# Bias rows of ada_b as single rows in zeroed tiles instead of 32 copies each

## The chip, the core and the metric

The kernel runs on one core of one Trainium2 chip. Its engines are TensorE (PE, with its weight loads PEld), VectorE (DVE), ScalarE (ACT), GpSimd (POOL) and SyncE (SP), which here issues every DMA. The metric is device time in microseconds (us) of one execution; the median of several executions is compared.

## What is computed

Two layers of a diffusion backbone, with 256 latent tokens and 256 context tokens of width 1024. Each layer is a half-step SwiGLU network, a token mixer (neighbourhood attention in layer 0, a short gated convolution in layer 1) and a second half-step network; the context is only carried as far as the attention needs it. Every sub-layer takes its shift, scale and gate from a modulation vector of the layer:

```
s_c, s_cc = silu(c), silu(c_ctx)
m  = (s_c  @ ada_w[i] + ada_b[i])        # 9 rows of 1024 for the latent tokens
mc = (s_cc @ ada_w[i] + ada_b[i])        # the same for the context
x  = layer_norm(alpha * x + w * gate * f(x * (1 + scale) + shift)) * g + b
```

`ada_w[i]` is 1024 x 9216 and `ada_b[i]` has 9216 entries, all in float32. The change is about how `ada_b` gets to the core.

## The kernel before

Matrices stream from DRAM in tiles, and each is split into a high part (ScalarE, line 178) and a low part (VectorE, line 181); three matmuls on these parts make one product. The order of TensorE's instructions is that of the program. The instructions of the other engines, and with them SP's queue of DMAs, are put in order by a planner at build time: it goes by the order in the text, shifted by the `high_priority` offsets, and by what it reckons to be ready.

The first modulation (rows 0 and 1 of layer 0) is worked out in `start_step`, before anything else can run, in five steps `(k0, n)` over column blocks of 128: (0, 1), (1, 1), (2, 2), (4, 2), (6, 2). A step loads its part of `ada_w` into tiles `ar` (line 478), loads x and the context (`x`, `xc`, line 485) when `k0` is even, multiplies by the silu of the two vectors (`ada`, line 490; `cst` holds the two vectors in columns 0 and 1 of 32, the others are zero), adds the bias tile `ab0` (`rows`, line 495), transposes x (`xT`, line 500), turns the rows into columns by a matmul with the selector `sel` (`mc`, line 522) and applies the modulation (lines 509 to 515). Between the pieces of a step stand the matmuls of the first panels of the network's first matrix (`f`, lines 537 to 539), whose tiles `w1r` are loaded at line 175.

`ab0` is two tiles of 128 x 512, cleared on VectorE (line 450). Half of the bias is loaded in step 0 and half in step 3, each time behind the step's last `ar` (line 481). Each of two rows of 512 entries is copied 32 times, to fill 64 partitions. The selector adds partitions 32m + v and 64 + 32m + v, for row m and vector v.

The other modulations are worked out beside the networks by `ada` (line 224), a background generator that is advanced by `tick`, a fraction of a step for each group of matmuls. A group has one or two vectors. For each of eight blocks of `ada_w`, VectorE multiplies and adds into the accumulators `acc` (lines 241 and 243); then the bias comes into `adab` (line 249), four ticks of work later TensorE sums over the partitions (line 259), VectorE adds the bias (line 260), and the result goes to the DRAM rows `scr` (line 262). From there `fold_cols` fetches it as `mrow`, and other code as `gate`. In `ada` too each of the two half rows of a vector is copied 32 times. The tag `acc` has four buffers of 512 columns, shared with `ab0` at the start; `adab` has one buffer.

Of the kernel before, what the change touches and what calls it, by code (L numbers as in the profile page):

```python
# [9 lines left out]
F32 = mybir.dt.float32  # L10
F32R = mybir.dt.float32r
AF = mybir.ActivationFunctionType
ALU = mybir.AluOpType
# [3 lines left out]
P = 128  # L17
D = 1024
# [46 lines left out]
def backbone_kernel(  # L65
# [6 lines left out]
    nc = tc.nc  # L72
    sync = nc.sync
# [7 lines left out]
    hp = phase.__enter__()  # L81
# [6 lines left out]
    def nm(s):  # L88
        uid[0] += 1
        return f"{s}_{uid[0]}"  # L90

    def act(dt=F32, s="a"):
        return ap.tile([P, 512], dt, tag="act", name=nm(s))
# [7 lines left out]
    def tpb(s="tp"):  # L101
        return bank("tp", s)
# [85 lines left out]
    def wpair(w, u, c0, c1, s):  # L188
        if c1 == c0 + 256:
# [22 lines left out]
    nc.vector.memset(ones, 1.0)  # L212
    sel = cp.tile([P, 4], F32, tag="sel", name="sel")
    idv = ident.rearrange("p (o m e) -> p o m e", o=2, m=2)
    nc.vector.tensor_tensor(out=sel.rearrange("p (m v) -> p m v", m=2), in0=idv[:, 0, :, 0:2],
                            in1=idv[:, 1, :, 0:2], op=ALU.add)
    win_sb = cp.tile([P, 64], F32, tag="wmask", name="wmask")
    rope = cp.tile([P, 2, 4, HD], F32, tag="rope", name="rope")

    scr = [tc.dram_tile([2, 9 * D], F32, name=f"scr{i}") for i in range(2)]  # L220
    xscr = tc.dram_tile([2 * P, D], F32, name="xscr")


    def ada(vecs):


        acc = {}
        for l, m in dict.fromkeys((l, m) for l, m, _ in vecs):
            for k in range(KC):
                w = hp.tile([P, D], F32, tag="ar", bufs=3, name=nm("ar"))  # L230
                sync.dma_start(w, ada_w[l, k * P:(k + 1) * P, m * D:(m + 1) * D])
                for i, vec in enumerate(vecs):
                    if vec[:2] != (l, m):
                        continue
                    if k == 0:
                        acc[i] = [hp.tile([P, 512], F32, tag="acc", bufs=4, name=nm("acc")) for _ in range(2)]
                    sc = cst[:, k, vec[2]:vec[2] + 1]
                    for h in range(2):
                        src, a = w[:, h * 512:(h + 1) * 512], acc[i][h]
                        if k == 0:  # L240
                            nc.vector.tensor_scalar(a, src, sc, None, op0=ALU.mult)
                        else:
                            nc.vector.scalar_tensor_tensor(out=a, in0=src, scalar=sc, in1=a,  # L243
                                                           op0=ALU.mult, op1=ALU.add)
                yield 1
        n = 2 * len(vecs)
        bt = hp.tile([P, 512], F32, tag="adab", name=nm("adab"))
        for i, (l, m, v) in enumerate(vecs):
            sync.dma_start(bt[64 * i:64 * i + 64],
                           bass.AP(ada_b.tensor, ada_b.offset + (l * 9 + m) * D, [[512, 2], [0, 32], [1, 512]]))  # L250
        yield 1
        yield 1
        yield 1
        rows = hp.tile([P, 512], F32, tag="adar", name=nm("adar"))
        ps = tpb("ada")
        for i in range(len(vecs)):
            for h in range(2):
                j = 2 * i + h
                nc.tensor.matmul(ps[32 * j:32 * j + 32, :], ones, acc[i][h], start=True, stop=True)
        nc.vector.tensor_tensor(out=rows[:32 * n], in0=ps[:32 * n], in1=bt[:32 * n], op=ALU.add)  # L260
        for i, (l, m, v) in enumerate(vecs):
            sync.dma_start(scr[l][v, m * D:(m + 1) * D].rearrange("(a b) -> a b", b=512),
                           rows[64 * i:64 * i + 64:32, :])
        yield 1

    def stream(*groups):
        for g in groups:
            yield from ada(g)
# [176 lines left out]


    w_in, w_out = ffn_w_in[0, 0], ffn_w_out[0, 0]
    ab0 = [hp.tile([P, 512], F32, tag="acc", bufs=4, name=nm("ab0")) for _ in range(2)]
    for h in range(2):
        nc.vector.memset(ab0[h], 0.0)  # L450
    xt = []
    for t in range(4):
        if t < 2:
# [9 lines left out]
    def start_tile():  # L463
        nar[0] += 1
        if nar[0] % 5 in (2, 4):
            return hp.tile([P, 2, 512], F32, tag="pt", bufs=4, name=nm("ar")).rearrange("p a b -> p (a b)")
        return hp.tile([P, D], F32, tag="ar", bufs=3, name=nm("ar"))

    def start_step(k0, n):

        ps = tpb("ada")
        m = n * P
        kt = 512 // m
        last = KC // kt - 1
        for a in range(KC // kt):
            w = start_tile().rearrange("p (k m c) -> p k m c", k=kt, m=2)
            for i in range(2):
                sync.dma_start(w[:, :, i], bass.AP(ada_w.tensor, ada_w.offset + a * kt * P * 9 * D + i * D + k0 * P,
                                                   [[9 * D, P], [P * 9 * D, kt], [1, m]]))
            if a == last and k0 % 4 == 0:  # L480
                sync.dma_start(ab0[k0 // 4][0:64], bass.AP(ada_b.tensor, ada_b.offset + k0 * P, [[D, 2], [0, 32], [1, 512]]))
            if a == (last if k0 else XAT) and k0 % 2 == 0:
                for t in range(4):
                    src = x[0] if t < 2 else ctxt[0]
                    sync.dma_start(xt[t][k0 // 4][:, k0 % 4 * P:k0 % 4 * P + 256],
                                   src[(t % 2) * P:(t % 2 + 1) * P, k0 * P:k0 * P + 256])
            for i in range(kt):
                for j in range(2):
                    o = 64 * (i % 2) + 32 * j
                    nc.tensor.matmul(ps[o:o + 32, 0:m], cst[:, a * kt + i, :], w[:, i, j, :],  # L490
                                     start=(a == 0 and i < 2), stop=(a == last and i >= kt - 2))
            if (a + 1) % (n if n == 1 else 2) == 0:
                yield
        rows = sp.tile([P, 256], F32, tag="s2", bufs=S2, name=nm("rows"))
        nc.vector.tensor_tensor(out=rows[:, 0:m], in0=ps[:, 0:m], in1=ab0[k0 // 4][:, k0 % 4 * P:k0 % 4 * P + m], op=ALU.add)

        def xT(k):
            px = tpb("xT")
            for t in range(4):
                nc.tensor.transpose(px[:, t * P:(t + 1) * P], xt[t][k // 4][:, (k % 4) * P:(k % 4 + 1) * P], ident)  # L500
            return px

        def mod(k, px):
            t = sp.tile([P, 512], F32, tag="s2", bufs=S2, name=nm("h"))
            hi, lo = act(F32R, "h0h"), act(F32R, "h0l")
            with tc.high_priority(offset=W_EARLY):
                for v in range(2):
                    s = slice(v * 256, (v + 1) * 256)
                    nc.scalar.activation(hi[:, s], px[:, s], AF.Identity, bias=mcol[:, k, 0, v:v + 1],
                                         scale=mcol[:, k, 1, v:v + 1])  # L510
                for v in range(2):
                    s = slice(v * 256, (v + 1) * 256)
                    nc.vector.tensor_scalar(t[:, s], px[:, s], mcol[:, k, 1, v:v + 1], mcol[:, k, 0, v:v + 1],
                                            op0=ALU.mult, op1=ALU.add)
                nc.vector.tensor_tensor(out=lo, in0=t, in1=hi.bitcast(F32), op=ALU.subtract)
            hT0.append((hi, lo))

        px = xT(k0)
        yield
        pc = tpb("mc")  # L520
        for i in range(n):
            nc.tensor.matmul(pc[:, 4 * i:4 * i + 4], rows[:, i * P:(i + 1) * P], sel, start=True, stop=True)
        pv = pc[:, 0:4 * n].rearrange("p (k m v) -> p k m v", k=n, m=2)
        nc.vector.tensor_copy(mcol[:, k0:k0 + n, 0, :], pv[:, :, 0, :])
        nc.vector.tensor_scalar(mcol[:, k0:k0 + n, 1, :], pv[:, :, 1, :], 1.0, None, op0=ALU.add)
        mod(k0, px)
        yield
        if n > 1:
            mod(k0 + 1, xT(k0 + 1))
            yield  # L530
# [23 lines left out]
    b1 = [mmb("f0", z) for z in range(2)]  # L554
    steps = ((0, 1), (1, 1), (2, 2), (4, 2), (6, 2))
    run(start_step(*steps[0]))
    for q, (k0, n) in enumerate(steps):
        nxt = start_step(*steps[q + 1]) if q < 4 else iter(())
        for g in range(6):
# [6 lines left out]
            p, j, z = g // 4, g // 2 % 2, g % 2  # L566
# [295 lines left out]
    hp = phase.__enter__()  # L862
# [67 lines left out]
    hTs, later = box  # L930
    phase = tc.tile_pool(name="ph2", bufs=1)
    hp = phase.__enter__()
    ext[0] = 3

    set_background(stream([(1, 1, 0), (1, 2, 0)], [(1, 3, 0)]), 0.35)
# [122 lines left out]
```

## Time and profile before

| what | value |
| --- | --- |
| median of 3 runs | 1293.48 us (1292.49 to 1294.41) |
| profiled execution | 1290.21 us |
| its span, first to last instruction | 1288.4 us |
| granted TensorE clock | 0.996 |
| DMA traffic | 271.26 MB, mean 211 GB/s |
| loads of `ab` | 2 of 128 KB |
| loads of `adab` | 19 of 128 KB |

The span leaves out what lies before the first and behind the last instruction, 1.8 us here. In the profile's rows, `L481` is a line of the kernel, `out<-in` names tiles and tensors without their numbers, `xN` is a count, and what stands in brackets or behind `<-` is the idle time ahead of it and what ended it. SPq rows are the issues of DMAs on SP, and their duration is that of the issue, not of the transfer.

### The profile page before, as it was taken

What the parts mean: (1) busy time and instruction counts of PE and PEld (TensorE: products, weight loads), DVE (VectorE), ACT (ScalarE), POOL (GpSimd) and SP (SyncE); (2) the same over time, 40 slices, a digit from 0 to 9 for tenths busy, and PEclk for the clock granted to TensorE, in tenths of its full rate; (3) what the DMA queues carried; (4) which work ended last, traced back from release to release, by engine and by line L of the source; (5) the groups of instructions that cost most, each with busy time, mean ns of one, the idle gap of its engine ahead of it and who ended that gap; (6) DMA issues with size and microseconds to landing.
All of it is one profiled execution on the core that took longest, in us unless ns stands there. A gap on an engine that the chain in (4) does not pass through costs nothing.

```text
span 1288.4 us, 17192 instructions
## 1 busy us (share of the span) xinstructions
PE 1256.5 (98%) x5890; PEld 1005.4 (78%) x5890; DVE 954.7 (74%) x1683; ACT 591.0 (46%) x1148; POOL 40.4 (3%) x69
## 2 busy tenths in 40 slices
PE   7999999999999999988999999999999999999997
PEld 4787778788778877766787787887788877788886
DVE  3599877595658767788997888867878688855545
ACT  2433132412326456677554535645435645655431
POOL 0000000000001111120000000000000000000000
PEclk9999999999999999989999999999999999999999
DMA  9978668484622744464998988677887764676641
GB/s 285 284 238 260 187 187 289 153 299 150 216 66 85 217 90 90 92 149 130 314 333 267 325 315 298 205 220 222 290 298 244 211 218 147 214 213 187 226 158 50
DMA packets 204018, 271.26 MB, mean 211 GB/s; under 512 B 30028, under 2 KB 149300, under 8 KB 203930
## 3 DMA queue, kind: packets, MB, share of 16 engines
q1 hardware_dynamic: 203930, 270.16, 66.9%
q8 instruction: 46, 0.75, 0.2%
q14 instruction: 42, 0.34, 0.1%
HBM read 267.93 MB, written 2.17 MB: 210 GB/s over the span
## 4 chain that ended last, share of the span: by engine, by line
PE 81%; DVE 7%; DMA 6%; ACT 3%; issue 1%; SPq 1%; POOL 0%; DVEq 0%; ACTq 0%
PE w L156 15%; PE w L157 14%; PE w L159 14%; PE f L537 6%; PE f L539 6%; PE f L538 6%; DMA w1r<-in_ffn_w_in_dram 4%; DVE w1l L181 2%; PE wkv L156 2%; PE wkv L159 2%; PE wkv L157 2%; PE wc L156 2%; PE wc L157 2%; PE wc L159 2%; DMA ar<-in_ada_w_dram 1%
## 5 line engine op out<-in xcount | busy, mean ns | idle before, releaser
L178 ACT ACTIVATE w1h<-w1r 128x512 fp32r<-128x512 f32 x352 | 203.1, 626 | 185.7 <-PE w L159 71.4
L181 DVE TENSOR_TENSOR w1l<-w1r,w1h 128x512 fp32r<-128x512 f32 x352 | 227.6, 685 | 66.7 <-ACT w1h L178 63.5
L156 PE MATMUL w<-w1h,hTh 128*128 128x512 f32 x528 | 210.8, 399 | 3.3 <-ACT hTh L105 3.3
L243 DVE SCALAR_TENSOR_TENSOR acc<-ar,cst,acc 128x512 f32<-128x512 f32 x266 | 187.5, 746 | 33.6 <-DMA ar<-in_ada_w_dram 33.3
L157 PE MATMUL w<-w1l,hTh 128*128 128x512 f32 x528 | 207.0, 392 | 0.0
L156 PE MATMUL w<-w2h,gh 128*128 128x512 f32 (+1 forms) x446 | 175.4, 394 | 0.0
L157 PE MATMUL w<-w2l,gh 128*128 128x512 f32 (+1 forms) x446 | 173.4, 389 | 0.0
L178 ACT ACTIVATE w2h<-w2r 128x512 fp32r<-128x512 f32 x176 | 101.5, 624 | 140.9 <-PE w L159 122.2
L159 PE MATMUL w<-w1h,hTl 128*128 128x512 f32 x528 | 163.4, 391 | 0.7 <-DVE hTl L106 0.7
L181 DVE TENSOR_TENSOR w2l<-w2r,w2h 128x512 fp32r<-128x512 f32 x176 | 114.0, 686 | 42.1 <-ACT w2h L178 41.4
L537 PE MATMUL f<-h0h,w1h 128*128 128x512 f32 x352 | 139.3, 396 | 0.0
L539 PE MATMUL f<-h0l,w1h 128*128 128x512 f32 x352 | 137.8, 392 | 0.0
L538 PE MATMUL f<-h0h,w1l 128*128 128x512 f32 x352 | 137.8, 391 | 0.0
L159 PE MATMUL w<-w2h,gl 128*128 128x512 f32 (+1 forms) x446 | 136.3, 387 | 0.0
L156 PEld LDWEIGHTS w<-w1h,hTh 128*128 128x128 f32 x528 | 99.2, 188 | 27.2 <-ACT hTh L105 4.6
L159 PEld LDWEIGHTS w<-w1h,hTl 128*128 128x128 f32 x528 | 98.9, 188 | 23.9 <-DVE hTl L106 1.5
L157 PEld LDWEIGHTS w<-w1l,hTh 128*128 128x128 f32 x528 | 99.2, 188 | 20.3 <-DVE w1l L181 0.3
L156 PEld LDWEIGHTS w<-w2h,gh 128*128 128x128 f32 x446 | 83.7, 188 | 21.8 <-issue 1.7
L159 PEld LDWEIGHTS w<-w2h,gl 128*128 128x128 f32 x446 | 83.3, 188 | 18.8
L157 PEld LDWEIGHTS w<-w2l,gh 128*128 128x128 f32 x446 | 83.7, 188 | 17.4
L537 PEld LDWEIGHTS f<-h0h,w1h 128*128 128x128 f32 x352 | 66.2, 188 | 17.9 <-issue 4.1
L539 PEld LDWEIGHTS f<-h0l,w1h 128*128 128x128 f32 x352 | 66.2, 188 | 14.4
(176 smaller groups left out, 1703.1 us busy)
## 6 DMA issues: line engine op xcount, KB each, us to landing
w1r<-in_ffn_w_in_dram SPq DMA_DIRECT2D x352, 256.0 KB
ar<-in_ada_w_dram SPq DMA_DIRECT2D x128, 512.0 KB
w2r<-in_ffn_w_out_dram SPq DMA_DIRECT2D x88, 512.0 KB
ar<-in_ada_w_dram SPq DMA_DIRECT2D x32, 256.0 KB
wkvr<-in_na_w_qkv_dram SPq DMA_DIRECT2D x32, 256.0 KB
wcr<-in_sc_w_in_dram SPq DMA_DIRECT2D x32, 256.0 KB
wqr<-in_na_w_qkv_dram SPq DMA_DIRECT2D x8, 512.0 KB
bias<-in_na_rpb_dram SPq DMA_DIRECT2D x64, 64.0 KB
```

Source lines behind the costliest of these rows:

```text
L156: nc.tensor.matmul(ps, lh, rh, start=first and i == 0, stop=False)
L157: nc.tensor.matmul(ps, lh, rl, start=False, stop=False)
L159: nc.tensor.matmul(ps, ll, rh, start=False, stop=last and i == n - 1)
L178: nc.scalar.activation(hi[:, a:a + m // W_HI], raw[:, a:a + m // W_HI], AF.Copy)
L181: nc.vector.tensor_tensor(out=lo[:, a:b], in0=raw[:, a:b], in1=hi[:, a:b].bitcast(F32), op=ALU.subtract)
L243: nc.vector.scalar_tensor_tensor(out=a, in0=src, scalar=sc, in1=a, op0=ALU.mult, op1=ALU.add)
L537: nc.tensor.matmul(ps, lh, hT0[k][0], start=(k == 0), stop=False)
L538: nc.tensor.matmul(ps, ll, hT0[k][0], start=False, stop=False)
L539: nc.tensor.matmul(ps, lh, hT0[k][1], start=False, stop=(k == KC - 1))
```

## The change

- `ab0` is one tile of 128 x 1024 with one clear. One DMA ahead of the loop over `start_step` puts bias row 0 into partition 2 and bias row 1 into partition 34, 1024 entries each. The loads at line 481 go.
- `sel` gets a second addition, by which partition 32m + 2 is added for both vectors. The matmul's rows 32m + 2 are zero, since column 2 of `cst` is zero, so what stands there is the bias alone.
- In `ada`, the bias goes into partitions 64i and 64i + 32 only, a row of 512 entries each. The tile `adab` is made and cleared (on GpSimd) once for each of the two phases that run `ada`, and is then used by all their groups.
- The accumulators, and `ab0` with them, are tiles of 1024 columns with two buffers, where there were four of 512.

```
+    sv = sel.rearrange("p (m v) -> p m v", m=2)
+    nc.vector.tensor_tensor(out=sv, in0=idv[:, 0, :, 0:2], in1=idv[:, 1, :, 0:2], op=ALU.add)
+    nc.vector.tensor_tensor(out=sv, in0=sv, in1=idv[:, 0, :, 2:3].to_broadcast([P, 2, 2]), op=ALU.add)
...
+    bias_rows = []
...
-                        acc[i] = [hp.tile([P, 512], F32, tag="acc", bufs=4, name=nm("acc")) for _ in range(2)]
+                        a = hp.tile([P, D], F32, tag="acc", bufs=2, name=nm("acc"))
+                        acc[i] = [a[:, 0:512], a[:, 512:D]]
...
-        bt = hp.tile([P, 512], F32, tag="adab", name=nm("adab"))
+        if not bias_rows:
+            bias_rows.append(hp.tile([P, 512], F32, tag="adab", name=nm("adab")))
+            nc.gpsimd.memset(bias_rows[0], 0.0)
+        bt = bias_rows[0]
         for i, (l, m, v) in enumerate(vecs):
-            sync.dma_start(bt[64 * i:64 * i + 64],
-                           bass.AP(ada_b.tensor, ada_b.offset + (l * 9 + m) * D, [[512, 2], [0, 32], [1, 512]]))
+            sync.dma_start(bt[64 * i:64 * i + 64:32], ada_b[l, m * D:(m + 1) * D].rearrange("(a b) -> a b", b=512))
...
-    ab0 = [hp.tile([P, 512], F32, tag="acc", bufs=4, name=nm("ab0")) for _ in range(2)]
-    for h in range(2):
-        nc.vector.memset(ab0[h], 0.0)
+    ab0 = hp.tile([P, D], F32, tag="acc", bufs=2, name="ab0")
+    nc.vector.memset(ab0, 0.0)
+    sync.dma_start(ab0[2:64:32], ada_b[0, 0:2 * D].rearrange("(m b) -> m b", m=2))
...
-            if a == last and k0 % 4 == 0:
-                sync.dma_start(ab0[k0 // 4][0:64], bass.AP(ada_b.tensor, ada_b.offset + k0 * P, [[D, 2], [0, 32], [1, 512]]))
...
-        nc.vector.tensor_tensor(out=rows[:, 0:m], in0=ps[:, 0:m], in1=ab0[k0 // 4][:, k0 % 4 * P:k0 % 4 * P + m], op=ALU.add)
+        nc.vector.tensor_tensor(out=rows[:, 0:m], in0=ps[:, 0:m], in1=ab0[:, k0 * P:k0 * P + m], op=ALU.add)
...
+    bias_rows.clear()
```

More of the change, by code (lines that the diff above doesn't have):

```diff
@@ L214, in backbone_kernel @@
     idv = ident.rearrange("p (o m e) -> p o m e", o=2, m=2)
-    nc.vector.tensor_tensor(out=sel.rearrange("p (m v) -> p m v", m=2), in0=idv[:, 0, :, 0:2],
-                            in1=idv[:, 1, :, 0:2], op=ALU.add)
+    sv = sel.rearrange("p (m v) -> p m v", m=2)
+    nc.vector.tensor_tensor(out=sv, in0=idv[:, 0, :, 0:2], in1=idv[:, 1, :, 0:2], op=ALU.add)
+    nc.vector.tensor_tensor(out=sv, in0=sv, in1=idv[:, 0, :, 2:3].to_broadcast([P, 2, 2]), op=ALU.add)
     win_sb = cp.tile([P, 64], F32, tag="wmask", name="wmask")
```

## The prediction

> **What bounds the kernel now.** I read the page first, then the busy time by stage, the waits of TensorE and of the DMA queue, and the start in order of time. From the page, the engines:
>
> ```profile
> PE 1256.5 (98%) x5890; PEld 1005.4 (78%) x5890; DVE 954.7 (74%) x1683; ACT 591.0 (46%) x1148; POOL 40.4 (3%) x69
> ```
>
> TensorE is busy for 1256.5 of 1288.4 us, so no change that leaves its matmuls alone can win more than the 31.9 us between. Where those lie is in the table by stage (window, its length, then busy us of PE, PEld, DVE, ACT and POOL, the granted clock, the DMA engines' share and GB/s):
>
> ```profile
> 5.00:10.00 5.00, 3.14 (x32) 1.35 (x30) 0.00 (x0) 0.00 (x0) 0.00 (x0) 1.00 0.99 279
> 10.00:15.00 5.00, 2.35 (x12) 1.48 (x16) 1.53 (x6) 1.88 (x4) 0.00 (x0) 1.00 0.89 271
> ...
> 35.00:40.00 5.00, 3.55 (x19) 2.41 (x19) 0.83 (x4) 1.24 (x3) 0.00 (x0) 1.00 0.76 226
> ...
> 100.00:200.00 100.00, 100.00 (x447) 79.38 (x446) 87.23 (x141) 25.68 (x44) 0.00 (x0) 1.00 0.70 215
> ```
>
> TensorE is idle for 1.86 + 2.65 us between 5 and 15, and for 1.45 us between 35 and 40: 6.0 us in all. In a later stage, as from 100 to 200, it is full. The waits of TensorE, over the whole run, name a transfer only in this start (the last column is the longest wait):
>
> ```profile
> PE ada L490 <- DMA ar<-in_ada_w_dram: 3.8, 4, 1.9
> PE xT L500 <- DMA x<-in_x_dram: 3.7, 2, 2.3
> ```
>
> So the start is bound by transfers, and the rest by TensorE. Which transfers decide is in the DMA queue's own rows, in order of time:
>
> ```profile
> 1.53 2.06 SPq L478 DMA_DIRECT2D ar<-in_ada_w_dram  x4
> 3.63 0.67 SPq L481 DMA_DIRECT2D ab<-in_ada_b_dram  x1
> 4.35 0.90 SPq L485 DMA_DIRECT2D x<-in_x_dram  x2
> 5.29 0.90 SPq L485 DMA_DIRECT2D xc<-in_ctx_dram  x2
> 6.23 0.43 SPq L175 DMA_DIRECT2D w1r<-in_ffn_w_in_dram  x1
> 6.81 0.38 SPq L478 DMA_DIRECT2D ar<-in_ada_w_dram  x1
> 7.58 0.37 SPq L175 DMA_DIRECT2D w1r<-in_ffn_w_in_dram  x1
> 10.65 0.37 SPq L478 DMA_DIRECT2D ar<-in_ada_w_dram  x1
> ...
> 28.09 0.56 SPq L481 DMA_DIRECT2D ab<-in_ada_b_dram  x1
> 28.76 1.09 SPq L485 DMA_DIRECT2D x<-in_x_dram  x2
> 30.18 1.09 SPq L485 DMA_DIRECT2D xc<-in_ctx_dram  x2
> 31.70 1.14 SPq L175 DMA_DIRECT2D w1r<-in_ffn_w_in_dram  x2
> 33.23 0.37 SPq L478 DMA_DIRECT2D ar<-in_ada_w_dram  x1
> 36.60 0.37 SPq L175 DMA_DIRECT2D w1r<-in_ffn_w_in_dram  x1
> ```
>
> SP issues nothing between 7.95 and 10.65, and nothing between 33.60 and 36.60. The waits say what held it, and what held VectorE beside it:
>
> ```profile
> SPq L175 <- DMA ab<-in_ada_b_dram: 2.9, 1, 2.9
> SPq L478 <- DMA ab<-in_ada_b_dram: 2.7, 1, 2.7
> ```
>
> ```profile
> DVE rows L495 <- DMA ab<-in_ada_b_dram: 12.4, 2, 8.5
> ```
>
> Both times it is `ab`, the 128 KB of bias that this change takes away. It takes 7.0 us from issue to landing (3.63 to 10.65) and then 8.5 us (28.09 to 36.60). Both times the issue that waits is the eighth after it, so SP seems to keep eight transfers in flight, and a late one blocks the line.
>
> Why is it so late? The DMA engines' share in short windows tells: alone, or draining, such a transfer keeps about 2 of the 16 engines busy (2/16 is 0.125):
>
> ```profile
> 36.80:37.60 0.80, 0.72 (x3) 0.42 (x3) 0.26 (x1) 0.00 (x0) 0.00 (x0) 1.00 0.19 64
> 1043.60:1044.00 0.40, 0.40 (x3) 0.35 (x2) 0.30 (x1) 0.40 (x2) 0.00 (x0) 1.00 0.12 41
> ```
>
> The second window follows a later `adab` transfer of the same form with nothing else moving: 0.12 and 41 GB/s. At that rate 131 KB last 3.2 us, on two engines that must carry their part of every other transfer too. The whole start then waits for these two: x lands behind the bias, and fourteen engines run dry.
>
> **The change, part by part.** For the sum I take the stages of the start and compare each with the rate that the DMA engines hold where no bias is in flight:
>
> ```profile
> 28.09:36.00 7.91, 7.12 (x51) 3.99 (x49) 4.40 (x8) 2.17 (x5) 0.00 (x0) 1.00 1.08 315
> 36.00:38.40 2.40, 1.50 (x9) 1.09 (x10) 0.42 (x1) 0.00 (x0) 0.00 (x0) 1.00 0.50 152
> 11.10:12.30 1.20, 1.20 (x6) 0.81 (x6) 0.00 (x0) 0.00 (x0) 0.00 (x0) 1.00 0.49 145
> 12.40:28.00 15.60, 13.92 (x108) 9.21 (x109) 7.18 (x18) 5.05 (x10) 0.00 (x0) 1.00 1.06 332
> ...
> 3.00:11.10 8.10, 3.53 (x33) 1.69 (x33) 0.29 (x1) 0.11 (x1) 0.00 (x0) 1.00 1.00 284
> ```
>
> The full rate is 332 GB/s. Time lost against it:
> - the hole after the first bias: 1.20 x (1 - 145/332) = 0.68 us
> - the hole after the second: 2.40 x (1 - 152/332) = 1.30 us
> - the slower stretch ahead of that hole: 7.91 x (1 - 315/332) = 0.41 us
> - the bytes that are no longer moved: 262 KB / 332 GB/s = 0.79 us
>
> Together 3.2 us. The last load that gates TensorE in the start is that of the last modulation step, where its weight load waits 0.35 us for `ar`:
>
> ```profile
> 45.75 1.45 PEld L490 LDWEIGHTS ada<-ar,cst 128*32 128x32 f32 x32 [0.35 <-DMA ar<-in_ada_w_dram]
> ```
>
> From there on TensorE waits for no transfer, so 3.2 us less of transfer time is 3.2 us less of span, if TensorE can follow. It can: it has 6.0 us of idle time to give. I take 3.2. The bounds: from above 3.2 plus what 3.00 to 11.10 lost, 8.10 x (1 - 284/332) = 1.2 us, so 4.4 us, if that stretch too was slow because of the bias and not because of its small pieces; from below the bytes alone, 0.8 us. I take no part of the 1.2, since the stretch is at a share of 1.00 and so has no hole.
>
> [...]
>
> What is added at the start:
>
> ```profile
> 1.22 1.02 DVE L450 MEMSET ab<- 128x512 f32 x2
> 2.16 0.10 DVE L215 TENSOR_TENSOR sel<-ident 128x4 f32<-128x4 f32 x1
> ```
>
> The two clears become one of twice the size, again 1.02 us. The added operation on `sel` is another 0.10 us in the 8.5 us in which VectorE then stands idle until the first bias lands; without that cover it would cost 0.10 us. The one bias load, 8 KB, has to wait for the clear, which ends at 2.24. If it stands first on SP, all of ada_w, x and the context are queued behind it: the first `ar` would go out at 2.24 plus about 0.5 us for the issue ahead of it (four `ar` take 2.06 us of SP), at 2.7 instead of 1.53: 1.2 us late. But the program is not queued as written: `sel` (line 215) stands ahead of the clears (line 450) in the text, and behind them in the trace, since `ident` wasn't ready. I expect the load to be passed by some `ar` in the same way, and the delay to be 0 to 1.2 us; I take 0, as the row of `sel` is the nearest, and keep 1.2 for a rival. As the issue of a large `ab` (0.67 us) goes from the same queue, SP's own work doesn't grow.
>
> In the streams, 19 `adab` loads of 128 KB become loads of 4 KB, and two clears of 128x512 go to GpSimd, which is busy 3% of the span: nothing, for GpSimd has 1248 us free and TensorE's waits name no `adab`. If that cover were gone, each clear would cost about the 0.51 us of one on VectorE. The wait of a next load for the reader of the shared tile stands in place of the wait for the old tile's release (one buffer each): nothing. The accumulators become one tile of 1024 columns with two buffers instead of four halves: same bytes, same operations, but see the second rival.
>
> Against the run: the profiled execution took 1290.21 us with a span of 1288.4; the median shown is 1293.48. I take the 3.2 us off the median: **1290.3 us**, or 1287.0 for an execution like the profiled one.
>
> **The rivals.**
> 1. *SP's front waits.* The small load stands ahead of ada_w and waits for the clear: 3.2 - 1.2 = 2.0 us won, 1291.5. For it: the text has it there, and SP serves in order. Against it: the row of `sel`.
> 2. *Slower: the accumulator in one piece.* A group's first multiplication may now have to wait until both halves of the old sum were read by TensorE. Among the idle times of VectorE ahead of its work on `acc`, in us and times, the trace has this wait twice:
>
> ```profile
>   PE ada L259: 1.4, 2
> ```
>
> With all 12 groups at 0.7 us it would be 8.4 us, 7.0 of them new, and the splits of the weights (`w1l`), and with them TensorE, queue behind it on VectorE. It decides where VectorE has no slack to make up for it; if all 7.0 us reach TensorE, the run takes 1293.5 - 3.2 + 7.0 = 1297.3. Against it: the stage from 100 to 200, in which several groups begin, has 12.8 us of VectorE idle.
> 3. *A transfer counts by its bytes.* The holes stay, because x and the context are late anyway: 0.8 us won, 1292.7. Against it: SP's two blocks are put down to `ab` and to nothing else. [...]
> 4. *The later loads count too.* The columns that fold the norms are fetched behind `adab` on the same engines, and TensorE waits for what they scale:
>
> ```profile
> PE w L156 <- ACT hTh L105: 3.3, 3, 2.0
> ```
>
> If all of that went as well, 3.2 + 3.3 = 6.5 us: 1287.0. Against it: the statistics of the norm end last there by the waits, not the columns.
>
> **How the numbers follow.** Forecast 0.50, its own range 1289.1 (4.4 won) to 1291.3; rival 1 0.18, rival 2 0.13, rival 3 0.09, rival 4 0.10. Within 0.2% is 1290.9 to 1296.1, about what a measurement of this kernel can tell from no change. The forecast lies close to that line: 0.38 of its 0.50 falls below it and 0.12 within. With rival 4 (0.10) and a little of rival 1 (0.02), faster has 0.50; the rest of rival 1 (0.16), rival 3 (0.09), 0.01 of rival 2 and that 0.12 make 0.38 for the same; slower has the other 0.12 of rival 2. The range from 1286.5 to 1295.5 takes in all cases but rival 2 and the tails that a new order of the planner may add on both sides.
>
> **What would show it.** Right: no stop of SP near 8 or 33 us; TensorE's 3.7 us of waiting for x are gone; no DMA share near 0.13 between 36 and 38; the last modulation step's matmuls begin near 42.5 instead of 45.75; TensorE then full to the same stages as before. Rival 1 shows in the first `ar` issued after 2.5 us, rival 2 in waits of `acc` for `ada` growing from 1.4 us, rival 4 in a smaller wait for `hTh`. Wrong it would be if the last step begins near 42.5 and the end does not move: then something later, not the start, sets it.

## The result, and the profile after

The changed kernel takes 1286.16 us (median of 6, 1285.67 to 1289.17) where the one before takes 1293.32 us on the same chip (median of 6, 1291.08 to 1294.63): ratio 0.9939 [0.9918, 0.9961], faster by 7.2 us. The forecast had 3.2 us and a range that ended at 1286.5. The two profiled executions differ by only 1.0 us of span (1288.4 and 1287.4), as before's was a short one (6 of 70 other runs of that kernel are shorter) and after's the longest of its six. So the traces are read here for what waits on what, and the sizes come from medians.

From the page of the kernel after, the engines: the same work, in a shorter time.

```profile
PE 1257.7 (98%) x5890; PEld 1007.0 (78%) x5890; DVE 955.1 (74%) x1683; ACT 591.2 (46%) x1148; POOL 42.0 (3%) x71
```

Its start by windows (columns as before: PE, PEld, DVE, ACT, POOL, clock, DMA share, GB/s):

```profile
10.00:15.00 5.00, 3.04 (x23) 1.96 (x21) 1.68 (x6) 2.06 (x4) 0.00 (x0) 1.00 1.10 328
...
35.00:40.00 5.00, 5.00 (x29) 4.24 (x28) 2.39 (x7) 3.22 (x7) 0.00 (x0) 1.00 0.98 302
```

And in the two windows that held the holes:

```profile
11.10:12.30 1.20, 0.26 (x2) 0.18 (x2) 0.16 (x2) 0.95 (x2) 0.00 (x0) 1.00 1.05 324
36.00:38.40 2.40, 2.40 (x16) 2.08 (x15) 0.79 (x4) 1.62 (x4) 0.00 (x0) 1.00 0.98 291
```

Both holes are filled: 324 GB/s where there were 145, and 291 where there were 152. From 35 to 40 us TensorE is full. SP's rows of the kernel after, in order of time, show why:

```profile
1.53 0.41 SPq L484 DMA_DIRECT2D ar<-in_ada_w_dram  x1
2.27 0.62 SPq L456 DMA_DIRECT2D ab<-in_ada_b_dram  x1
2.93 1.50 SPq L484 DMA_DIRECT2D ar<-in_ada_w_dram  x3
4.47 0.98 SPq L489 DMA_DIRECT2D x<-in_x_dram  x2
5.49 0.90 SPq L489 DMA_DIRECT2D xc<-in_ctx_dram  x2
6.44 0.43 SPq L175 DMA_DIRECT2D w1r<-in_ffn_w_in_dram  x1
6.92 1.02 SPq L484 DMA_DIRECT2D ar<-in_ada_w_dram  x2
8.63 1.39 SPq L175 DMA_DIRECT2D w1r<-in_ffn_w_in_dram  x3
10.07 7.51 SPq L484 DMA_DIRECT2D ar<-in_ada_w_dram  x10
...
30.14 1.34 SPq L175 DMA_DIRECT2D w1r<-in_ffn_w_in_dram  x2
32.71 0.37 SPq L484 DMA_DIRECT2D ar<-in_ada_w_dram  x1
33.44 0.37 SPq L175 DMA_DIRECT2D w1r<-in_ffn_w_in_dram  x1
```

The stops of 2.7 and 3.0 us near 8 and 34 us are gone; the longest that is left in these rows is one of 1.2 us, at 31.5. Among TensorE's waits in the kernel after, none names the load of x any more; these two, which stood beside it, are no smaller than they were (5.3 for 3.8, 3.7 for 3.3):

```profile
PE ada L494 <- DMA ar<-in_ada_w_dram: 5.3, 5, 1.7
PE w L156 <- ACT hTh L105: 3.7, 3, 2.7
```

The last step's matmuls begin at 43.75 us, 2.0 earlier than in the profiled execution before:

```profile
43.75 2.01 PE L494 MATMUL ada<-ar,cst 128*32 128x256 f32 x32
```

### The profile page after: what moved, and what is told of

Its sections match the earlier page's. It is cut to its first block, busy times and chain, and to the rows that moved or that the text cites. A ratio compares the mean times of both kernels' runs of the same rounds, so it can differ in the third digit from the quotient of the medians.

```text
span 1287.4 us, 17193 instructions
## 1 busy us (share of the span) xinstructions
PE 1257.7 (98%) x5890; PEld 1007.0 (78%) x5890; DVE 955.1 (74%) x1683; ACT 591.2 (46%) x1148; POOL 42.0 (3%) x71
## 4 chain that ended last, share of the span: by engine, by line
PE 78%; DVE 8%; DMA 8%; ACT 3%; issue 2%; SPq 1%; POOL 0%; DVEq 0%; ACTq 0%
PE w L156 13%; PE w L157 13%; PE w L159 13%; PE f L541 6%; PE f L542 6%; PE f L543 6%; DMA ar<-in_ada_w_dram 5%; DMA w1r<-in_ffn_w_in_dram 2%; PE wkv L156 2%; PE wkv L157 2%; PE wkv L159 2%; PE wc L156 2%; PE wc L157 2%; PE wc L159 2%; DVE w1l L181 2%
```

## The experiments

Two questions: is it the few engines of the old loads (a share of 0.12 of the 16 in the kernel before, where one such load moved alone from 1043.60 to 1044.00 us) that cost the time, or their bytes; and is it the start alone, or the 19 later loads too.

**Engines or bytes.** `spread_one` keeps all copies and bytes and exchanges two steps of the source of each of the 21 bias loads, so that the slowest dimension has 32 entries and not 2:

```
-  bass.AP(ada_b.tensor, ..., [[512, 2], [0, 32], [1, 512]])      # adab; for ab: [[D, 2], [0, 32], [1, 512]]
+  bass.AP(ada_b.tensor, ..., [[0, 32], [512, 2], [1, 512]])      # adab; for ab: [[0, 32], [D, 2], [1, 512]]
```

> The kernel before, with the two slowest steps of each bias load's source exchanged, so that its slowest dimension is 32 and not 2; same bytes, same instructions in the same order on every engine. Half of the filled partitions get the other one of the two rows, so a wrong bias is added. Theory (the gain is that two DMA engines no longer carry 64 KB each): most of the 7 us, 5 to 7 us faster than before, and SP no longer stops near 8 and near 33 us. Rival (bytes alone, 2.75 MB fewer): nothing, within 1 us of before. Rival (the accumulators in one piece, or the order of the queues): nothing, as neither is changed.

It took 1288.07 us, ratio 0.9944 [0.9924, 0.9963], close to the whole change with none of its bytes saved. In its SP rows the second load of `ab` is followed by others without a long stop (its waits name `ab` once, for 0.3 us):

```profile
28.71 0.56 SPq L485 DMA_DIRECT2D ab<-in_ada_b_dram  x1
29.31 1.06 SPq L489 DMA_DIRECT2D x<-in_x_dram  x2
30.51 1.05 SPq L489 DMA_DIRECT2D xc<-in_ctx_dram  x2
31.88 1.42 SPq L175 DMA_DIRECT2D w1r<-in_ffn_w_in_dram  x2
34.08 0.37 SPq L482 DMA_DIRECT2D ar<-in_ada_w_dram  x1
34.62 0.37 SPq L175 DMA_DIRECT2D w1r<-in_ffn_w_in_dram  x1
```

**Start or later loads.** `start_only` is the change with `adab` as before; `late_only` the reverse; `acc_only` is before with nothing but the tiles of 1024 columns:

```
# start_only, in ada: a new tile for each group, and
+  sync.dma_start(bt[64 * i:64 * i + 64], bass.AP(ada_b.tensor, ..., [[512, 2], [0, 32], [1, 512]]))
# late_only, acc_only, in start_step:
+  sync.dma_start(ab0[0:64, k0 * P:k0 * P + 512], bass.AP(ada_b.tensor, ..., [[D, 2], [0, 32], [1, 512]]))
```

> The changed kernel with the loads of adab as before (32 copies, a new tile each). Theory: the start's 2 us, as the last step of the first modulation begins 2.0 us earlier in the changed kernel's profile (43.75 against 45.75); 1.5 to 3 us faster than before. Rival (accumulators or order): the whole 7 us, since both are as in the changed kernel. Rival (the start's idle time is all that counts): 7 us as well.

1288.54 us, 0.9954 [0.9937, 0.9971]: some 6 us, twice what the theory allowed and short of the whole.

> The kernel before in its start (two loads of 128 KB into one tile, behind the step's weights), with the loads of adab as single rows into a tile cleared once. Theory (the 19 later loads count too, through stages that transfers bound): 4 to 6 us faster than before. Rival (only the start counts): within 1 us of before. Its start should still show SP's two stops.

1291.8 us, 0.9981 [0.9964, 0.9998]: some 2.4 us, between the two expectations, with an interval that ends just below no change. In its start SP still stops for `ab` twice, for 2.4 and 2.3 us.

> The kernel before with the accumulators, and the first bias tile, as tiles of 1024 columns with two buffers; all loads as before. Theory: within 1 us of before. Rival 2 of the prediction (waiting for both halves): up to 7 us slower. Rival (this is what won the 5 us that the start doesn't explain): 4 to 6 us faster.

1292.23 us, 0.9993 [0.9974, 1.0012]: no difference seen. To see whether the late part is real, `start_only` and the change ran again, as `start_again` and `after_again`:

> The changed start with the later loads as before, once more, beside the changed kernel on one chip. Theory (the 19 later loads count as well): 1.5 to 3 us above the changed kernel. Rival (only the start counts): within 1 us of it.

> The changed kernel once more, beside the changed start alone. About 0.994 of the kernel before, as in its first comparison; what it stands for is the difference to the changed start alone.

1288.48 us, 0.9953 [0.9935, 0.9971], and 1286.46 us, 0.9945 [0.9925, 0.9966]. The intervals overlap, but with both rounds together the means are 1288.33 us (19 runs) and 1286.48 us (13 runs): the later loads are worth 1.84 +- 1.28 us (95%). The second round alone, in which both ran on one chip, gives 1.90 +- 1.81.

**Which of the later loads.** `late_ph0` loads single rows in the first networks and 32 copies behind the attention (8 loads); `late_ph2` does the reverse, with 11 loads as copies in the first networks:

```
-        if not bias_rows:
+        one = ext[0] != 3          # late_ph2: ext[0] == 3
+        ... the single rows and the shared, cleared tile only where one is true
```

> The changed kernel, but with the later bias loads after the attention (8 of 19) as before, 32 copies of each row; the rest as in the changed kernel. Theory (they cost where transfers bound the networks after the attention): 1.5 to 3 us above the changed kernel (1286.3), at 1288 to 1289. Rival (they cost in the first network): within 1 us of the changed kernel.

> The changed kernel, but with the 11 later bias loads of the first network as before. Theory (TensorE has no idle time from 40 to 480 us, so nothing is lost there): within 1 us of the changed kernel (1286.3). Rival: 1.5 to 3 us above it.

1287.75 us, 0.997 [0.9954, 0.9985], and 1285.51 us, 0.9951 [0.9933, 0.9968]. The means of the runs are 1288.44 and 1286.09, 2.34 +- 2.30 us apart: `late_ph0` is like `start_only`, `late_ph2` like the full change. The interval only just leaves out zero, so the runs alone point to the loads behind the attention rather than prove them. The traces say more, and show which of them it is. The first group there has two vectors, and so two loads in a row. SP's rows at that place, in the kernel before:

```profile
669.94 1.17 SPq L249 DMA_DIRECT2D adab<-in_ada_b_dram  x2
671.22 15.34 SPq L175 DMA_DIRECT2D w1r<-in_ffn_w_in_dram  x12
```

In the kernel after:

```profile
668.03 1.21 SPq L256 DMA_DIRECT2D adab<-in_ada_b_dram  x2
669.48 10.72 SPq L175 DMA_DIRECT2D w1r<-in_ffn_w_in_dram  x12
```

And in `late_ph2`:

```profile
667.34 1.10 SPq L256 DMA_DIRECT2D adab<-in_ada_b_dram  x2
668.56 10.47 SPq L175 DMA_DIRECT2D w1r<-in_ffn_w_in_dram  x12
```

Twelve issues of `w1r` take 15.3 us behind the copies and 10.5 to 10.7 behind single rows: the block of the start once more. VectorE then waits for ScalarE's `w1h`, which is made from `w1r`; its next row in the kernel before:

```profile
682.93 2.72 DVE L181 TENSOR_TENSOR w1l<-w1r,w1h 128x512 fp32r<-128x512 f32 x4 [4.41 <-ACT w1h L178]
```

And in the kernel after:

```profile
679.78 0.69 DVE L181 TENSOR_TENSOR w1l<-w1r,w1h 128x512 fp32r<-128x512 f32 x1 [0.48 <-ACT w1h L178]
```

4.41 us against 0.48. VectorE catches up with most of it, but some 10 and 25 us later TensorE waits for `sil`, which VectorE makes. Over the whole run, in the kernel before:

```profile
PE gT L394 <- DVE sil L386: 0.9, 2, 0.6
```

In the kernel after:

```profile
PE gT L400 <- DVE sil L392: 0.3, 1, 0.3
```

And in order of time in `late_ph0`:

```profile
693.92 0.77 PE L400 MATMUL gT<-ident,sil 128*128 128x128 f32 x4 [0.45 <-DVE sil L392]
707.48 0.44 PE L400 MATMUL gT<-ident,sil 128*128 128x128 f32 x2 [1.46 <-DVE sil L392]
```

In all five traces with copies in the old form at that place (before, `acc_only`, `start_only`, `start_again`, `late_ph0`) the twelve issues take 14.5 to 15.7 us, and this wait of TensorE's sums to 0.9, 1.9, 1.2, 1.4 and 1.9 us. In all six others (`spread_one` among them) they take 10.5 to 11.7 us, and the wait is 0.3 us in the kernel after and absent from the rest. It is the largest part of the 1.84 us that the traces show.

Not every such stop costs time. SP waits for `adab` at a second place, at 82 us, in the first networks; in the kernel before and in `late_ph2`:

```profile
SPq L944 <- DMA adab<-in_ada_b_dram: 2.9, 1, 2.9
SPq L949 <- DMA adab<-in_ada_b_dram: 3.1, 1, 3.1
```

`late_ph2` keeps this stop and is as short as the full change.

**The start by itself.** Whole runs scatter by several us, so four kernels stop behind the first modulation and its matmuls and leave everything after it out:

```
+    for i, bk in enumerate(b0[0] + b0[1]):
+        ... four accumulated tiles to out
+    return
```

> The kernel before cut off behind the first modulation and its matmuls: four banks of the first panels' sums go to the output, everything later is left out. It measures the start by itself, over many executions. In single profiles the last multiplication of the first modulation ended at 47.3 (before), 48.4 and 50.0 us (two kernels with the same start), so 57 to 65 us are expected here. Its difference to the cut version of the changed kernel is what tells the theories apart.

73.72 us (72.65 to 75.86).

> The changed kernel, cut in the same way. Theory (the whole gain lies in the start, and single profiles show too little of it): 6 to 7 us less than the cut kernel before. Rival (the start gives the 3.2 us forecast, the rest is won later by the 19 smaller loads): about 3 us less.

69.13 us (68.58 to 69.31): the start is worth 4.6 us, between the two expectations. The four shortest of `t_before`'s seven runs have a median of 73.17; by them it is 4.0. The two longest were at a low clock, which is taken up below.

> The kernel before, cut in the same way, with the two steps of the bias loads' source exchanged (slowest dimension 32, same bytes and order of queues; half of the filled partitions get the wrong row). Theory (two engines): within 1 us of the cut changed kernel. Rival (bytes): within 1 us of the cut kernel before.

69.91 us: 3.8 of the 4.6 go with the order of the source's steps, at the same bytes (3.2 of the 4.0); single rows, with the other edits of the change, bring 0.8 more.

> The changed kernel, cut in the same way, with its one small bias load behind the first step's weights on SP instead of second among them, where it waited 0.33 us for the clear (SP idle from 1.94 to 2.27). If that wait sits on the path, 0.3 to 0.9 us (the wait, and the issue of 0.62 us) less than the cut changed kernel; if transfers bound the start anyway, nothing.

This is the change with its small load not ahead of ada_w but behind the first step's part of it:

```
-    sync.dma_start(ab0[2:64:32], ada_b[0, 0:2 * D].rearrange("(m b) -> m b", m=2))
...
+            if a == last and k0 == 0:
+                sync.dma_start(ab0[2:64:32], ada_b[0, 0:2 * D].rearrange("(m b) -> m b", m=2))
```

68.53 us (68.22 to 69.79), 0.6 us less than `t_after`, but the runs of the two overlap and the means are only 0.28 us apart. In `t_before` two of seven runs were long, 75.15 and 75.86 us, both at a mean granted clock of 0.95; the others have 0.967 to 1.0. The profiled one is among the long ones. TensorE's rows in order of time show its stop ahead of the second x:

```profile
37.50 0.53 PE L504 MATMUL xT<-ident,x 128*128 128x128 f32 x2 [1.84 <-DMA x<-in_x_dram]
38.07 0.85 PE L504 MATMUL xT<-ident,xc 128*128 128x128 f32 x2
...
40.42 0.63 PE L543 MATMUL f<-h0l,w1h 128*128 128x512 f32 x1
...
45.33 0.39 PE L541 MATMUL f<-h0h,w1h 128*128 128x512 f32 x1
```

The windows around it:

```profile
35.60:37.50 1.90, 0.06 (x2) 0.04 (x1) 0.24 (x1) 0.00 (x0) 0.00 (x0) 1.00 0.63 165
37.50:38.00 0.50, 0.50 (x2) 0.24 (x2) 0.18 (x1) 0.00 (x0) 0.00 (x0) 1.00 0.13 43
...
38.20:38.40 0.20, 0.20 (x1) 0.00 (x1) 0.00 (x0) 0.00 (x0) 0.00 (x0) 0.59 1.08 113
38.40:45.00 6.60, 6.59 (x21) 5.49 (x21) 3.75 (x9) 3.84 (x8) 0.00 (x0) 0.50 0.97 286
...
45.00:45.20 0.20, 0.20 (x2) 0.12 (x2) 0.20 (x2) 0.20 (x1) 0.00 (x0) 0.84 1.10 369
```

Some 0.7 us after the stop the granted clock (third number from the right) falls to 0.50 and stays there until 45.1; a matmul of 512 columns takes 0.63 us instead of 0.39. Three more kernels asked how much of the start is this clock. `t_before_fill` puts six more matmuls ahead of the transposes of x in the fourth step:

```
+            for i in range(6 if k == 4 else 0):
+                nc.tensor.matmul(px, hT0[i % 2][0][:, 0:P], hT0[i % 2][0], start=True, stop=True)
```

> The cut kernel before, with six extra matmuls of 512 columns (about 1.4 us of TensorE) where it stands idle for x in the step of columns 4 and 5; their result is overwritten, the loads and all queues but TensorE's are as before. Theory (part of the start's loss is the clock: after that idle time the granted clock fell to 0.50 for 3 to 6 us in two profiles of three, and stayed at 1.00 in the profiled run before): the clock stays at 1.00 there and the median falls by 1 to 2.5 us from 73.7, towards what the transfers alone explain, 69.1 + 3.2 = 72.3. Rival (transfers alone set the start): no change or up to 1.4 us longer.

73.47 us (72.81 to 74.2) at clocks of 0.989 to 1.0: no long run is left among six, and the shortest are not shorter. Two long runs of seven against none of six can still be chance. It settles little: the added matmuls took 1.5 us themselves and began only at 37.18 in its profile, so they cost about what the clock would have. `t_fix_first` and `t_fix_second` are `t_before` with the source steps of only one of the two loads exchanged, as in `spread_one`:

```
+  [[0, 32], [D, 2], [1, 512]] if k0 == 0 else [[D, 2], [0, 32], [1, 512]]     # t_fix_second: if k0 != 0
```

> [...] Theory (the second load's stop near 36 us costs the larger part, the clock's fall with it): 72 us, and the granted clock still at 0.95 in some executions. Rival (the first load costs most, as everything starts later): 70 to 71 us and no low clocks.

> [...] Theory: 70.5 to 71.5 us, no execution with a mean clock of 0.95, no wait for x near 36 us. Rival: 72 us or more, and low clocks in some executions.

71.18 and 71.17 us: each takes 2.5 us off, both together 3.8 (`t_spread`). With the other load's steps already exchanged, each still takes 1.3 off (69.91). So the rival expected for `t_fix_first` comes nearer than the theory: the second load's stop isn't the larger part. The two ran on another chip than `t_before`; the kernel before took 1292.61 us there and 1293.06 here. The low clock didn't appear in the six runs of `t_fix_first`, though a stop of 1.2 us is left there at 36 us.

**A better place.** The whole change with the small load placed as in `t_behind`:

> The whole changed kernel with its first bias load behind the first step's weights on SP. The cut version of it was 0.6 us shorter than the cut changed kernel (68.53 against 69.13). Expected 0 to 1 us below the changed kernel, if the start reaches the end; no difference that can be seen otherwise.

1283.11 us (1282.76 to 1286.71), 0.9924 [0.9901, 0.9947]: shorter than both kernels, and than `after_again` on the same chip by 2.57 +- 1.79 us in the means. Its first rows of SP have no wait at the front:

```profile
1.52 2.05 SPq L482 DMA_DIRECT2D ar<-in_ada_w_dram  x4
3.62 0.62 SPq L485 DMA_DIRECT2D ab<-in_ada_b_dram  x1
4.28 0.89 SPq L489 DMA_DIRECT2D x<-in_x_dram  x2
```

## Why the prediction was right in kind and too small

**Where the time is lost** (right). The start was bound by two loads on few of the 16 DMA engines, by the share of 0.12, which held SP for 2.7 and 2.9 us. `spread_one` shows it for the whole kernel, where the same bytes without that form are 0.56% faster, and `t_spread` for the start by itself, 3.8 us. From 36.00 to 38.40 us, where the DMA engines' share was 0.50 in the kernel before, it is 1.05 in `spread_one`; how many engines the exchanged load itself runs on is not shown. For these loads, time by bytes alone, which is rival 3, is refuted, since only 0.8 us of the start's 4.6 are left for the bytes and the other edits.

**The sum of 3.2 us** (mis-sized: 4.6 measured, 4.0 by the shorter runs). The bytes' term, 0.79, stands against 0.8, by luck in part: the front wait below is in the 0.8 too. The others, 2.4 in all, came out at 3.8 (3.2). The one at fault is that of the first load: 0.68 us, from the hole at 11.10 alone, where removing this load's form gives 2.5 us alone and 1.3 on top of the second. The second load's terms, 1.30 + 0.41, lie between its 1.3 and 2.5. The stretch from 3.00 to 11.10 was left out because its DMA share was 1.00. In the kernel after:

```profile
3.00:11.10 8.10, 4.40 (x38) 2.78 (x38) 0.36 (x2) 0.12 (x1) 0.00 (x0) 1.00 0.94 280
```

The bytes go no faster than before (280 GB/s for 284), but TensorE is busy for 4.40 us where it was 3.53. In `t_before` and `t_fix_second`, with the first load in the old form too, it is 3.61 and 3.39 us; in `start_again`, `t_after` and `load_behind`, without it, 4.10, 4.70 and 4.77. So the share of 1.00 there did not say that the engines carried what was waited for. The upper bound, 4.4, had that stretch in it, but as a rate that would rise to 332 GB/s, and it did not rise.

**A term that was missing: the clock.** In the profiled execution before, the stop at 36 us left the clock at 1.00, so no step of the sum had it. In `t_before`, the runs at 1.0 have a mean of 73.2 us and the two at 0.95 one of 75.5: 2.3 us when it happens. Against the median of 73.72 it is some 0.5 us of the 4.6. In whole runs the time goes with the mean granted clock too: over 70 runs of the kernel before, 1.24 us for each 0.001 of it (correlation -0.71), and the mean clock is 0.9959 there against 0.9964 in the 13 runs of the change, which would be 0.6 us. That the change raised it is not shown: in those 13 runs the correlation is only -0.36, low stretches lie elsewhere too (0.50 from 560.00 to 565.00 us in the profile before, 0.66 from 800.00 to 805.00 in the one after), and `start_again`, which has the changed start, shows 0.78 from 12.40 to 28.00 us, which is 6.9 us at 0.50 if the rest was at 1.00. How long a stop it takes is not shown: the clock fell after one of 1.84 us in `t_before` and one of 1.66 us in `acc_only`, and stayed at 1.00 after one of 2.3 us at 11 us in the profile before. Nor is what ends a low stretch: the one in `t_before` lasted 6.8 us (38.24 to 45.06, from the 0.59 and 0.84 above), with TensorE busy for 6.59 of the 6.60 us shown, and the one in `acc_only` 3.4 us (39.83 to 43.24, in the same way from 0.79 between 39.60 and 40.00 and 0.69 between 42.00 and 44.00).

**SP's front wait, taken as 0** (nearly; rival 1 in part). One `ar` passed the load, and the first went out at 1.53 as forecast. But the load went second, not later, and SP stands idle ahead of it, from 1.94 to 2.27 us; from SP's waits in the kernel after:

```profile
SPq L456 <- DVE sel L217: 0.5, 1, 0.5
```

The name is not to be taken at its word here. VectorE's rows:

```profile
1.33 0.91 DVE L455 MEMSET ab<- 128x1024 f32 x1 [0.16 <-issue]
2.30 0.16 DVE L217 TENSOR_TENSOR sel<-sel,ident 128x4 f32<-128x4 f32 x1
```

The clear ends at 2.24, just ahead of the issue, and the operation on `sel` begins only behind it. So it is the clear, as forecast, with 0.33 us of waiting and 0.62 of issue ahead of the second `ar`. What that costs is 0.6 us by the medians of `t_behind`, which is not clear of scatter, and the last step begins at 42.61 us in `load_behind`, near the 42.5 that was forecast for a front without wait, against 43.75 and 43.08 in the two profiles of the change. In whole runs the better place gives 2.57 +- 1.79 us. Its mean clock is 0.9975 against 0.9964, 1.4 us by the slope above; whether the rest is scatter stays open.

**The 19 later loads, taken as nothing** (wrong, and the step that failed). The reason given was that TensorE's waits name no `adab`. They don't; but SP's waits in the profile before do, and nothing in the prediction followed them:

```profile
SPq L175 <- DMA adab<-in_ada_b_dram: 2.7, 1, 2.7
```

It is the very wait that was read for `ab` at the start. It reached TensorE three steps later, by `w1r`, `w1h`, VectorE's order and `sil`. Rival 4 guessed that these loads count, but put it into the waits for `hTh`, which went from 3.3 to 3.7 us and did not shrink. Of the 1.84 us, the traces' waits for `sil` explain 0.6 to 1.9; the other 17 loads show nothing that can be told from scatter.

**The accumulator in one piece** (rival 2: refuted). Before its work on `acc` VectorE waits for `ada` twice, as before, for 2.6 us instead of 1.4, in the kernel after:

```profile
  PE ada L265: 2.6, 2
```

The other groups don't wait, and `acc_only` is at 0.9993.

**The whole.** 4.6 us of the start and 1.84 us of the later loads are 6.4, against 7.2 (0.9939 [0.9918, 0.9961]) and `after_again`'s 0.9945. Of the 4.0 us that the forecast missed, the later loads are 1.84, the start 0.8 to 1.4, and the rest has no owner. In whole runs the start alone reads larger, some 6 us by `start_only` and `start_again` (0.9954 and 0.9953); their intervals, 2.2 us to either side, don't tell that from 4.6.

## What to carry to other kernels

Don't judge a small DMA by its bytes alone; look at the order of its source's steps too: exchanging two source steps of the 128 KB bias loads, with nothing else changed, made this kernel 0.56% faster. Where a queue has stopped on a load in one place, look for the same form in its other waits, and follow what was queued behind it through the engines, even if the bound engine's waits never name it; whether the stop costs anything is decided by the slack behind it (the one of 3.1 us at 82 us in `late_ph2` cost nothing that its runs show). And take a size from many runs: two profiled spans differed by 1.0 us where the medians differ by 7.2.

## What was not expected of the hardware

- A stop of 1.84 us ahead of transposes and small matmuls was followed by 6.8 us at a granted clock of 0.50 (`t_before`), one of 1.66 by 3.4 us (`acc_only`), one of 1.22 (`t_fix_first`) and two of 2.3 and 1.42 (the kernel before) by none.
- Two loads of 128 KB in the old form lengthened the issue of the next twelve from some 10.5 us to 15.3.
- The kernel before runs between 1288.3 and 1300.7 us over 70 executions, and 1.24 us of it goes with each 0.001 of the mean granted clock.
- With the first load in the old form, the DMA engines moved as many bytes per second from 3.00 to 11.10 us as without (284 and 280 GB/s), and TensorE was busy for 0.9 us less.
